# Differential attention in a hybrid diffusion block: a combination split between two engines and placed later, and products with v over two query tiles

## Chip, core and metric

One NeuronCore of a Trainium2 chip runs the whole program. The metric is the device time in microseconds. The engines are TensorE (PE, and PEld for its weight loads), VectorE (DVE), ScalarE (ACT), GpSimd (POOL) and SyncE (SP, which issues most DMAs).

## The reference

Two layers of a transformer block run over 1024 latent tokens and 256 context tokens (model width 1024). Each layer has three parallel head groups, an output projection and a gated MLP. The change lies in the first head group, differential attention: 4 heads, each with two score maps (m = 0, 1) over keys of width 32 and values of width 64.

```python
s = jnp.einsum('bqhmd,bkhmd->bhmqk', qb, keys).astype(F32) * scale
p = jax.nn.softmax(s, axis=-1)
w = p[:, :, 0] - lam * p[:, :, 1]
return jnp.einsum('bhqk,bkhd->bqhd', w.astype(vals.dtype), vals)
```

Latent queries see all 1280 keys. Context queries see the 256 context keys alone, and are needed in layer 0 only. An RMS norm per head follows, so the weights w may carry any common factor of a query.

## The kernel before

`Build.da` (line 860) runs the differential attention of a layer in steps. A step is one head and one tile of 128 queries: 4 heads times 10 tiles, 40 steps, in layer 0 (8 of them small, the context tiles), and 4 times 8, 32 steps, in layer 1. Tiles come in blocks (context tiles 8 and 9; tiles 0 to 3; tiles 4 to 7), heads in two pairs.

One step passes through these functions, with queries on the partitions until the transposes:

- `scores` (L890, matmul L901), once per map: scores of 128 queries against 1280 keys (256 in a small step) go into a PSUM buffer of three banks; there are two such buffers.
- `maximum` (L903, L911) on VectorE reads the buffer and gives the negated row maximum. `exps` (L913, L918) on ScalarE writes the exponentials to SBUF and accumulates their sum; then the PSUM buffer is free.
- `combine` (L922) on VectorE: the reciprocal of the second sum (L929), the ratio (L930), then w = e0 + ratio * e1 over all columns (L931), in place. The result is the difference of the two softmaxes times the first sum, which the norm takes out again.
- `transpose` (L933): TensorE transposes w in chunks of 128 keys (L942), up to four to a PSUM bank, and ScalarE copies each group of up to 512 columns into the tile `da_w` (L943). A large step has groups of 4, 4 and 2 chunks, a small one a single group of 2.
- `products` (L945): for each chunk a matmul with v as weights and the transposed w as 128 moving columns (`pv_mm`, L742); even and odd chunks go to two halves of the partitions of `da_pv`.
- `finish` (L954) calls `pv_combine` (L744): ScalarE copies one half to SBUF (L749) and VectorE adds the other half into the block's output `da_o` (L750). After the last tile of a block's second head `sub_norm` (L1096) starts the norm.

The loop at L963 writes the order by hand: in round n it writes the combination of step n-1, the products of step n-2, the maxima and exponentials of step n, `finish` of step n-2, other work from `plan[n]`, the first scores of step n+1, the transposes of step n-1 and the second scores of step n+1. A scheduler then orders each engine's instructions by priority and readiness, so the order in the trace can differ a little from the written one. Each engine executes its own queue strictly in order.

`fill_plan` (L1008) lays two other kinds of work into the steps: matrix-vector products for the modulation (`mod_units`, L302, L330, L291 to L296) and pieces of the output projection of the third head group (L1040: matmuls L1048 to L1050, ScalarE L1054, and an addition on GpSimd, L1056). These, the transposes, the products and the norm share two PSUM banks (`ps_t`, L205). At two places in a layer `load` fetches q and k of the other head pair by DMAs on GpSimd's queue (L856, L857). GpSimd also computes low-order parts of weights and activations (`lo`, L186) and the norm's power (L1111).

SBUF tiles come from pools: the exponentials from a pool of 7 (tag `x`), the transposed weights `da_w` from one of 6 (tag `wt`), and small work tiles from one of 6 (tag `s5`).

Of the kernel before, what the change touches and what calls it, by code (L numbers as in the profile page):

```python
# [11 lines left out]
F32 = mybir.dt.float32  # L12
F32R = mybir.dt.float32r
AF = mybir.ActivationFunctionType
ALU = mybir.AluOpType
# [6 lines left out]
P = 128  # L22
# [148 lines left out]
class Build:  # L171
# [688 lines left out]
    def da(self, pss, todo):  # L860
# [3 lines left out]
        nc, sp = self.nc, self.sp  # L864
# [20 lines left out]
        ns = len(steps)  # L885
# [17 lines left out]
        def maximum(n, mi):  # L903
            u, ti = steps[n]
            st, b = state[n], u["blk"]
            if mi == 0:
                st["sm"] = sp.tile([P, 8], F32, tag="sm", name="da_sm", bufs=8)
                if u["hd"] == 0 and ti == 0:
                    b["s0"] = sp.tile([P, 4, 2, 2], F32, tag="s0", name="da_s0", bufs=5)
                    b["o"] = self.s5("da_o")  # L910
            nc.vector.tensor_reduce(st["sm"][:, mi:mi + 1], st["s"][mi][:, :b["nkc"]], AX.X, ALU.max, negate=True)  # L911

        def exps(n, mi):  # L913
            u, ti = steps[n]
            st, b = state[n], u["blk"]
            nkc = b["nkc"]
            e = self.x_tile("da_e")
            nc.scalar.activation(e[:, :nkc], st["s"][mi][:, :nkc], AF.Exp, bias=st["sm"][:, mi:mi + 1],  # L918
                                 accum_out=b["s0"][:, ti, u["hd"], mi:mi + 1])
            st["e"].append(e)  # L920

        def combine(n):  # L922

            u, ti = steps[n]
            st, b = state[n], u["blk"]
            sm, (w, e1) = st["sm"], st["e"]
            s01 = b["s0"][:, ti, u["hd"], :]
            nkc = b["nkc"]
            nc.vector.reciprocal(sm[:, 4:5], s01[:, 1:2])  # L929
            nc.vector.scalar_tensor_tensor(sm[:, 5:6], s01[:, 0:1], self.nlam, sm[:, 4:5], ALU.mult, ALU.mult)  # L930
            nc.vector.scalar_tensor_tensor(w[:, :nkc], e1[:, :nkc], sm[:, 5:6], w[:, :nkc], ALU.mult, ALU.add)  # L931

        def transpose(n):  # L933
            u, ti = steps[n]
            st, b = state[n], u["blk"]
            w = st["e"][0]
            wt = st["wt"] = self.wt_tile("da_w", F32)
            for c in range(0, b["nk"], 4):
                n4 = min(4, b["nk"] - c)
                pt = self.ps_t("da_t")  # L940
                for i in range(n4):
                    nc.tensor.transpose(pt[:, P * i:P * i + P], w[:, P * (c + i):P * (c + i) + P], self.ident)  # L942
                nc.scalar.activation(wt[:, P * c:P * (c + n4)], pt[:, :P * n4], AF.Copy)  # L943

        def products(n):  # L945
            u, ti = steps[n]
            st, b = state[n], u["blk"]
            hd, nk = u["hd"], b["nk"]
            pv = st["pv"] = self.ps_t("da_pv")[:, :P]
            for c in range(nk):  # L950
                self.pv_mm(pv, c, nk, loaded[b["pair"]]["v"][:, b["kt0"] + c, 64 * hd:64 * hd + 64],
                           st["wt"][:, P * c:P * c + P])

        def finish(n):  # L954
            u, ti = steps[n]
            b = u["blk"]
            self.pv_combine(u["hd"], state[n]["pv"], b["o"][:, P * ti:P * ti + P], P)
            if u["hd"] == 1 and ti == len(b["tiles"]) - 1:
                late.append(self.sub_norm(b))

        scores(0, 0)
        scores(0, 1)
        for n in range(ns + 2):  # L963
            if n == ns // 4 + 3:
                load(1, (0, 1))
            if n == ns // 2 + 3:
                load(1, (2, 3))
            if n == ns - 10:
                for k in range(2, KE):
                    self.y_load(k, "h")  # L970
            if n == ns - 4:
                self.y_split(2, nc.scalar, nc.gpsimd)
            if n == ns - 3:
                self.y_split(3, nc.scalar, nc.gpsimd)
            prev, new, out = 1 <= n <= ns, n + 1 < ns, n >= 2
            if prev:
                combine(n - 1)
            if out:
                products(n - 2)
            if n < ns:  # L980
                maximum(n, 0)
            if n < ns:
                exps(n, 0)
            if n < ns:
                maximum(n, 1)
            if n < ns:
                exps(n, 1)
            if out:
                finish(n - 2)
            if n < ns:  # L990
                for fn in plan[n]:
                    fn()
            if new:
                scores(n + 1, 0)
            if prev:
                transpose(n - 1)
            if new:
                scores(n + 1, 1)
            late = [g for g in late if next(g, True) is None]
            if n == ns - 2:  # L1000
                self.wo = [self.weight(self.a["wo"][self.l, 0], KE * P)]
# [768 lines left out]
```

## Time and profile before

| what | us |
|---|---|
| runs shown (3): median, lowest, highest | 3108.84, 3102.79, 3114.64 |
| profiled execution: its own time, and its span | 3104.49, 3102.60 |
| differential attention of layer 0 / layer 1, as windows of the span | 480 to 731 / 2127 to 2330 |
| busy over the span: PE, DVE, ACT, POOL | 2845.3, 2109.1, 1457.5, 1497.3 |
| mean granted TensorE clock, as a share of 2.4 GHz | 0.972 |

Engines overlap, so busy times add up to more than the span. A matmul's end is modelled, and matmuls are pipelined, so a busy TensorE is not one at its peak. A row of a group gives line, engine, operation, output <- inputs, shapes, count, then busy us, mean ns of one, and the idle time of the engine just before them with what ended it. A row of the timeline gives start, duration, and in brackets idle time before it. A row of the waits names who waited for whom, the total in us, how often, and the longest.

### The profile page before, as it was taken

The numbers are of one execution on the slowest core, as the hardware profiler recorded it, in microseconds if no ns is written. First come the engines' busy times: TensorE is split into PE (matmuls) and PEld (weight loads), VectorE is DVE, ScalarE is ACT, GpSimd is POOL, SyncE is SP. The second block draws the span as 40 slices with busy tenths as digits, with TensorE's granted clock in tenths as the row PEclk, the third lists the DMA queues.
The fourth block names the chain that finished last, engine by engine and source line by source line (L and its number), as shares of the span: only waits on it lengthen the run. The fifth ranks groups of instructions, "written<-read, shape, count | busy, mean of one in ns | idle before, by whom it ended". The sixth has DMA issues, their size and how long they took to land. (4 is left out here: it accounts for less than half of the span.)

```text
span 3102.6 us, 41077 instructions
## 1 busy us (share of the span) xinstructions
PE 2845.3 (92%) x15194; PEld 2307.3 (74%) x15194; DVE 2109.1 (68%) x2979; ACT 1457.5 (47%) x2442; POOL 1497.3 (48%) x971
## 2 busy tenths in 40 slices
PE   6899798999899999998988989798989799998898
PEld 4798665667688888887877778666767678887676
DVE  6956577875855444457887875767885755555997
ACT  5444367775444333343322454467873444444331
POOL 4645402223455444439561664602323566665981
PEclk9999899999999999999999999899999999999999
DMA  7232816654121121143215331454434122224322
GB/s 251 83 93 68 202 27 228 204 197 149 59 80 67 67 75 67 67 174 118 82 57 206 92 108 52 123 121 146 134 110 166 55 82 82 82 82 163 121 84 82
DMA packets 207577, 349.27 MB, mean 113 GB/s; under 512 B 32784, under 2 KB 112400, under 8 KB 207376
## 3 DMA queue, kind: packets, MB, share of 16 engines
q1 hardware_dynamic: 202768, 331.69, 33.2%
q0 software_dynamic: 4608, 14.95, 2.2%
q8 instruction: 120, 1.97, 0.3%
q14 instruction: 81, 0.66, 0.1%
HBM read 257.19 MB, written 89.39 MB: 112 GB/s over the span
## 5 line engine op out<-in xcount | busy, mean ns | idle before, releaser
L184 ACT ACTIVATE w_r<-w_raw 128x512 fp32r<-128x512 f32 x338 | 212.7, 631 | 449.7 <-PE u_ps L1518 280.1
L1490 POOL TENSOR_TENSOR w_raw<-w_raw 128x512 f32<-128x512 f32 x176 | 250.3, 1427 | 227.5 <-DVE w_r L187 102.8
L187 DVE TENSOR_TENSOR w_r<-w_raw,w_r 128x512 fp32r<-128x512 f32 x206 | 150.4, 732 | 251.5 <-ACT w_r L184 251.4
L187 POOL TENSOR_TENSOR w<-raw,w 128x1024 fp32r<-128x1024 f32 (+2 forms) x62 | 142.9, 2311 | 318.2 <-ACT w L184 207.1
L1517 PE MATMUL u_ps<-a,w_r 128*128 128x512 f32 x704 | 278.6, 396 | 5.3 <-DVE vb L1605 4.2
L1518 PE MATMUL u_ps<-a,w_r 128*128 128x512 f32 x704 | 277.8, 395 | 1.4 <-DVE a L187 1.2
L1519 PE MATMUL u_ps<-a,w_r 128*128 128x512 f32 x704 | 276.2, 392 | 0.0
L187 POOL TENSOR_TENSOR w_r<-w_raw,w_r 128x512 fp32r<-128x512 f32 x132 | 190.4, 1442 | 119.9 <-ACT w_r L184 114.7
L1369 PE MATMUL d_ps<-d_ah,d_b 128*128 128x512 f32 x560 | 223.1, 399 | 22.5 <-DVE xd L1346 11.1
L1370 PE MATMUL d_ps<-d_al,d_b 128*128 128x512 f32 x560 | 222.8, 398 | 9.0 <-DVE d_al L187 9.0
L1371 PE MATMUL d_ps<-d_ah,d_b 128*128 128x512 f32 x560 | 221.8, 396 | 0.7 <-DVE d_b L187 0.7
L911 DVE TENSOR_REDUCE da_sm<-da_s 128x1 f32<-128x1280 f32 (+1 forms) x144 | 195.5, 1368 | 34.1 <-PE da_s L901 32.7
L918 ACT ACTIVATE da_e<-da_s,da_sm 128x1280 f32<-128x1280 f32 (+1 forms) x144 | 177.5, 1235 | 23.7 <-DVE da_sm L911 20.6
L1056 POOL TENSOR_TENSOR oy_x<-oy_x,oy_z 128x426 f32<-128x426 f32 (+3 forms) x48 | 52.7, 1099 | 223.5 <-ACT oy_z L1054 191.7
L1517 PEld LDWEIGHTS u_ps<-a,w_r 128*128 128x128 f32 x704 | 133.8, 190 | 35.0 <-DVE vb L1605 5.7
L1518 PEld LDWEIGHTS u_ps<-a,w_r 128*128 128x128 f32 x704 | 133.9, 190 | 29.5 <-DVE a L187 2.0
L1519 PEld LDWEIGHTS u_ps<-a,w_r 128*128 128x128 f32 x704 | 133.7, 190 | 28.7
L1346 DVE SCALAR_TENSOR_TENSOR xd<-d_ps,mods,xd 128x512 f32<-128x512 f32 x200 | 141.0, 740 | 20.4 <-PE d_ps L1371 20.3
L1369 PEld LDWEIGHTS d_ps<-d_ah,d_b 128*128 128x128 f32 x560 | 107.6, 192 | 48.5 <-issue 9.4
L901 PE MATMUL da_s<-dak,daq 96*128 96x512 f32 (+1 forms) x400 | 125.2, 399 | 17.6 <-ACT da_e L918 17.4
L1605 DVE TENSOR_TENSOR vb<-u_ps,vb 128x512 f32<-128x512 f32 x96 | 66.1, 688 | 98.7 <-PE u_ps L1519 89.1
L1370 PEld LDWEIGHTS d_ps<-d_al,d_b 128*128 128x128 f32 x560 | 108.0, 193 | 32.0 <-DVE d_al L187 10.3
(347 smaller groups left out, 8635.6 us busy)
## 6 DMA issues: line engine op xcount, KB each, us to landing
wmod<-in_wmod SPq DMA_DIRECT2D x96, 512.0 KB, 6.4
w_raw<-in_wu SPq DMA_DIRECT2D x44, 1024.0 KB, 5.4
d_w<-in_wd SPq DMA_DIRECT2D x40, 512.0 KB, 3.9
d_a<-ud SPq DMA_DIRECT2D x40, 512.0 KB, 4.7
ud<-conv SPq DMA_DIRECT2D x22, 640.0 KB, 2.9
ud<-conv SPq DMA_DIRECT2D x22, 512.0 KB, 2.6
raw<-in_wg SPq DMA_DIRECT2D x16, 512.0 KB, 4.3
dak<-qk_da POOLq DMA_DIRECT2D x48, 160.0 KB, 8.1
```

The lines of the kernel that those rows point to most:

```text
L184: self.nc.scalar.activation(out, in_, AF.Copy)
L187: (eng or self.nc.vector).tensor_tensor(out, in_, hi.bitcast(F32), ALU.subtract)
L911: nc.vector.tensor_reduce(st["sm"][:, mi:mi + 1], st["s"][mi][:, :b["nkc"]], AX.X, ALU.max, negate=True)
L918: nc.scalar.activation(e[:, :nkc], st["s"][mi][:, :nkc], AF.Exp, bias=st["sm"][:, mi:mi + 1], accum_out=b["s0"][:, ti, u["hd"], mi:mi + 1])
L1346: nc.vector.scalar_tensor_tensor(x, ps, gate, x, ALU.mult, ALU.add)
L1369: nc.tensor.matmul(ps, bh[:, w], ah[:, m], start=on is None and k == 0, stop=False, **kw)
L1370: nc.tensor.matmul(ps, bh[:, w], al[:, m], start=False, stop=False, **kw)
L1371: nc.tensor.matmul(ps, bl[:, w], ah[:, m], start=False, stop=k == 1, **kw)
L1490: sub = lambda o, a, b, op=ALU.subtract: nc.gpsimd.tensor_tensor(o, a, b, op)
L1517: nc.tensor.matmul(ps, wh[:, s], h, start=new and kk == 0, stop=False, skip_group_check=not new)
L1518: nc.tensor.matmul(ps, wh[:, s], lo, start=False, stop=False, skip_group_check=not new)
L1519: nc.tensor.matmul(ps, wl[:, s], h, start=False, stop=kk == 3, skip_group_check=not new)
```

## The change

The three instructions of `combine` become two functions. `ratio` holds the reciprocal and the ratio. The new `combine` gives VectorE all columns but the last 512 and GpSimd the last 512, as a scaling of e1 and an addition; a small step stays wholly on VectorE. Both are written behind the maxima and exponentials of the following step instead of ahead of them, and the transposes of a step follow one round later. The transposed weights of two neighbouring query tiles lie side by side in one tile (chunks 0 to 7 in `da_w`, the rest in a work tile `da_w2`), so that a matmul of `products` moves 256 columns and serves both tiles; products and `finish` run every second round. The last group of a step's transposes (two chunks) is copied by VectorE instead of ScalarE.

```diff
--- before.py
+++ after.py
@@ -919,48 +919,71 @@
                                  accum_out=b["s0"][:, ti, u["hd"], mi:mi + 1])
             st["e"].append(e)
 
-        def combine(n):
+        def ratio(n):
 
             u, ti = steps[n]
             st, b = state[n], u["blk"]
-            sm, (w, e1) = st["sm"], st["e"]
+            sm = st["sm"]
             s01 = b["s0"][:, ti, u["hd"], :]
-            nkc = b["nkc"]
             nc.vector.reciprocal(sm[:, 4:5], s01[:, 1:2])
             nc.vector.scalar_tensor_tensor(sm[:, 5:6], s01[:, 0:1], self.nlam, sm[:, 4:5], ALU.mult, ALU.mult)
-            nc.vector.scalar_tensor_tensor(w[:, :nkc], e1[:, :nkc], sm[:, 5:6], w[:, :nkc], ALU.mult, ALU.add)
-
-        def transpose(n):
+
+        def combine(n):
+
             u, ti = steps[n]
             st, b = state[n], u["blk"]
-            w = st["e"][0]
-            wt = st["wt"] = self.wt_tile("da_w", F32)
-            for c in range(0, b["nk"], 4):
-                n4 = min(4, b["nk"] - c)
+            w, e1 = st["e"]
+            nkc, c = b["nkc"], st["sm"][:, 5:6]
+            h = nkc - 512 if nkc > 512 else nkc
+            nc.vector.scalar_tensor_tensor(w[:, :h], e1[:, :h], c, w[:, :h], ALU.mult, ALU.add)
+            if h < nkc:
+                nc.gpsimd.tensor_scalar(e1[:, h:nkc], e1[:, h:nkc], c, None, ALU.mult)
+                nc.gpsimd.tensor_tensor(w[:, h:nkc], w[:, h:nkc], e1[:, h:nkc], ALU.add)
+
+        def transpose(n):
+
+            u, ti = steps[n]
+            st, b = state[n], u["blk"]
+            w, nk = st["e"][0], b["nk"]
+            i = ti % 2
+            if i == 0:
+                st["wt"] = [self.wt_tile("da_w", F32)[:, 0:256 * min(nk, 8)].rearrange("p (c q) -> p c q", q=256)]
+                if nk > 8:
+                    st["wt"].append(self.s5("da_w2").rearrange("p (c q) -> p c q", q=256))
+            else:
+                st["wt"] = state[n - 1]["wt"]
+            for c in range(0, nk, 4):
+                n4 = min(4, nk - c)
                 pt = self.ps_t("da_t")
-                for i in range(n4):
-                    nc.tensor.transpose(pt[:, P * i:P * i + P], w[:, P * (c + i):P * (c + i) + P], self.ident)
-                nc.scalar.activation(wt[:, P * c:P * (c + n4)], pt[:, :P * n4], AF.Copy)
+                for k in range(n4):
+                    nc.tensor.transpose(pt[:, P * k:P * k + P], w[:, P * (c + k):P * (c + k) + P], self.ident)
+                dst = st["wt"][c // 8][:, c % 8:c % 8 + n4, P * i:P * i + P]
+                src = pt[:, :P * n4].rearrange("p (c q) -> p c q", q=P)
+                if n4 == 2:
+                    nc.vector.tensor_scalar(dst, src, 1.0, None, ALU.mult)
+                else:
+                    nc.scalar.activation(dst, src, AF.Copy)
 
         def products(n):
+
             u, ti = steps[n]
             st, b = state[n], u["blk"]
             hd, nk = u["hd"], b["nk"]
-            pv = st["pv"] = self.ps_t("da_pv")[:, :P]
+            pv = st["pv"] = self.ps_t("da_pv")[:, :2 * P]
             for c in range(nk):
                 self.pv_mm(pv, c, nk, loaded[b["pair"]]["v"][:, b["kt0"] + c, 64 * hd:64 * hd + 64],
-                           st["wt"][:, P * c:P * c + P])
+                           st["wt"][c // 8][:, c % 8, :])
 
         def finish(n):
             u, ti = steps[n]
             b = u["blk"]
-            self.pv_combine(u["hd"], state[n]["pv"], b["o"][:, P * ti:P * ti + P], P)
+            self.pv_combine(u["hd"], state[n]["pv"], b["o"][:, P * ti - P:P * ti + P], 2 * P)
             if u["hd"] == 1 and ti == len(b["tiles"]) - 1:
                 late.append(self.sub_norm(b))
 
         scores(0, 0)
         scores(0, 1)
-        for n in range(ns + 2):
+        for n in range(ns + 3):
             if n == ns // 4 + 3:
                 load(1, (0, 1))
             if n == ns // 2 + 3:
@@ -972,29 +995,28 @@
                 self.y_split(2, nc.scalar, nc.gpsimd)
             if n == ns - 3:
                 self.y_split(3, nc.scalar, nc.gpsimd)
-            prev, new, out = 1 <= n <= ns, n + 1 < ns, n >= 2
-            if prev:
+
+            out = n >= 4 and n % 2 == 0
+            if out:
+                products(n - 3)
+            if n < ns:
+                maximum(n, 0)
+                maximum(n, 1)
+                exps(n, 0)
+                exps(n, 1)
+            if 1 <= n <= ns:
+                ratio(n - 1)
                 combine(n - 1)
             if out:
-                products(n - 2)
-            if n < ns:
-                maximum(n, 0)
-            if n < ns:
-                exps(n, 0)
-            if n < ns:
-                maximum(n, 1)
-            if n < ns:
-                exps(n, 1)
-            if out:
-                finish(n - 2)
+                finish(n - 3)
             if n < ns:
                 for fn in plan[n]:
                     fn()
-            if new:
+            if n + 1 < ns:
                 scores(n + 1, 0)
-            if prev:
-                transpose(n - 1)
-            if new:
+            if 2 <= n <= ns + 1:
+                transpose(n - 2)
+            if n + 1 < ns:
                 scores(n + 1, 1)
             late = [g for g in late if next(g, True) is None]
             if n == ns - 2:
```

## Rows read from the trace of the kernel before

**Rows 1.** Busy time of each engine (with instruction counts), granted clock and DMA share, both stages.
```profile
core 0: us, PE busy (x) PEld busy (x) DVE busy (x) ACT busy (x) POOL busy (x), PEclk, DMA share, GB/s
480.00:731.00 251.00, 229.18 (x1731) 164.40 (x1733) 199.61 (x292) 191.33 (x371) 75.26 (x62) 0.98 0.60 192
2127.00:2330.00 203.00, 181.63 (x1485) 142.19 (x1483) 168.92 (x216) 163.35 (x296) 60.19 (x59) 0.98 0.47 138
```

**Rows 2.** VectorE's groups by shape, layer 0: busy us, mean ns | idle before, releasers.
```profile
L911 DVE TENSOR_REDUCE da_sm<-da_s 128x1 f32<-128x1280 f32 x64 | 94.7, 1487 | 16.4 <-PE da_s L901 15.7
L931 DVE SCALAR_TENSOR_TENSOR da_e<-da_e,da_sm 128x1280 f32<-128x1280 f32 x32 | 53.3, 1667 | 0.8
L750 DVE TENSOR_TENSOR da_o<-da_pv,pvt 64x128 f32<-64x128 f32 x40 | 11.5, 287 | 11.5 <-ACT pvt L749 10.1
L930 DVE SCALAR_TENSOR_TENSOR da_sm<-da_s,nlam,da_sm 128x1 f32<-128x1 f32 x40 | 11.2, 280 | 0.9
```

**Rows 3.** The same view, stage of layer 1: the combination.
```profile
L931 DVE SCALAR_TENSOR_TENSOR da_e<-da_e,da_sm 128x1280 f32<-128x1280 f32 x32 | 53.2, 1662 | 0.9
```

**Rows 4.** Timeline of VectorE in layer 1, one step: start us, duration us.
```profile
2148.84 0.16 DVE L929 RECIPROCAL da_sm<-da_s 128x1 f32<-128x1 f32 x1
2149.14 0.28 DVE L750 TENSOR_TENSOR da_o<-da_pv,pvt 64x128 f32<-64x128 f32 x1
2149.35 0.20 DVE L930 SCALAR_TENSOR_TENSOR da_sm<-da_s,nlam,da_sm 128x1 f32<-128x1 f32 x1
2149.59 1.55 DVE L931 SCALAR_TENSOR_TENSOR da_e<-da_e,da_sm 128x1280 f32<-128x1280 f32 x1
2151.05 2.88 DVE L911 TENSOR_REDUCE da_sm<-da_s 128x1 f32<-128x1280 f32 x2
2154.08 0.16 DVE L929 RECIPROCAL da_sm<-da_s 128x1 f32<-128x1 f32 x1
```

**Rows 5.** Waits in layer 0: who for whom, total us, times, longest.
```profile
DVE da_sm L911 <- PE da_s L901: 20.3, 23, 2.1
DVE da_sm L929 <- ACT da_e L918: 11.8, 14, 1.8
```

**Rows 6.** Waits in layer 1, the same view.
```profile
DVE da_sm L911 <- PE da_s L901: 12.4, 12, 3.7
DVE da_sm L929 <- ACT da_e L918: 8.1, 8, 1.5
```

**Rows 7.** VectorE's groups of the whole span: prices for the operations added.
```profile
L803 DVE TENSOR_SCALAR sw_w<-sw_t 128x512 f32<-128x512 f32 x32 | 22.0, 686 | 3.9 <-PE sw_t L794 3.9
L803 DVE TENSOR_SCALAR sw_w<-sw_t 128x256 f32<-128x256 f32 x4 | 1.7, 425 | 1.1 <-PE sw_t L794 1.1
L750 DVE TENSOR_TENSOR sw_yo<-sw_pv,pvt 64x384 f32<-64x384 f32 x36 | 20.0, 554 | 32.6 <-ACT pvt L749 32.6
```

**Rows 8.** Groups of ScalarE, then of TensorE, layer 0: group copies, products with v.
```profile
L943 ACT ACTIVATE da_w<-da_t 128x256 f32<-128x256 f32 x39 | 15.0, 386 | 2.5 <-PE da_t L942 2.2
L742 PE MATMUL da_pv<-da_w,v 128*64 128x128 f32 x672 | 46.5, 282 | 4.1 <-ACT da_w L943 3.5
```

**Rows 9.** GpSimd's groups by shape, the whole span.
```profile
L1490 POOL TENSOR_TENSOR w_raw<-w_raw 128x512 f32<-128x512 f32 x176 | 250.3, 1427 | 227.5 <-DVE w_r L187 102.8 <-DMA w_raw<-in_wu 78.0 <-PE c_ps L1530 37.2
L578 POOL TENSOR_SCALAR av<-av 128x1280 f32<-128x1280 f32 x12 | 17.9, 1491 | 60.6 <-DVE av L577 58.8 <-DVE qv L658 1.8
```

**Rows 10.** Timelines of VectorE and GpSimd where the two meet, layer 1.
```profile
2144.41 1.55 DVE L931 SCALAR_TENSOR_TENSOR da_e<-da_e,da_sm 128x1280 f32<-128x1280 f32 x1
2144.60 2.14 POOL L1056 TENSOR_TENSOR oy_x<-oy_x,oy_z 128x342 f32<-128x342 f32 x1 [0.26 <-ACT oy_z L1054]
2151.07 0.92 POOL L1056 TENSOR_TENSOR oy_x<-oy_x,oy_z 128x342 f32<-128x342 f32 x1 [4.33 <-ACT oy_z L1054]
2289.24 3.74 DVE L931 SCALAR_TENSOR_TENSOR da_e<-da_e,da_sm 128x1280 f32<-128x1280 f32 x1
2289.27 2.37 POOL L187 TENSOR_TENSOR yl<-yld,yh 128x1024 fp32r<-128x1024 f32 x1 [2.83 <-PE mod_ps L302]
```

More of the change, by code (lines that the diff above doesn't have):

```diff
@@ L920, in exps @@
             st["e"].append(e)
+        def ratio(n):
+            u, ti = steps[n]
+            st, b = state[n], u["blk"]
+            sm = st["sm"]
+            s01 = b["s0"][:, ti, u["hd"], :]
+            nc.vector.reciprocal(sm[:, 4:5], s01[:, 1:2])
+            nc.vector.scalar_tensor_tensor(sm[:, 5:6], s01[:, 0:1], self.nlam, sm[:, 4:5], ALU.mult, ALU.mult)
         def combine(n):
@@ L925, in combine @@
             st, b = state[n], u["blk"]
-            sm, (w, e1) = st["sm"], st["e"]
-            s01 = b["s0"][:, ti, u["hd"], :]
-            nkc = b["nkc"]
-            nc.vector.reciprocal(sm[:, 4:5], s01[:, 1:2])
-            nc.vector.scalar_tensor_tensor(sm[:, 5:6], s01[:, 0:1], self.nlam, sm[:, 4:5], ALU.mult, ALU.mult)
-            nc.vector.scalar_tensor_tensor(w[:, :nkc], e1[:, :nkc], sm[:, 5:6], w[:, :nkc], ALU.mult, ALU.add)
+            w, e1 = st["e"]
[5 more added lines that the diff above has]
+                nc.gpsimd.tensor_tensor(w[:, h:nkc], w[:, h:nkc], e1[:, h:nkc], ALU.add)
         def transpose(n):
```

## The prediction

> **What bounds the kernel now.** I read the windows first, to see how full each engine is in the two stretches that the change touches. In 480 to 731 us (layer 0) TensorE, VectorE and ScalarE show 229, 200 and 191 us of 251; in 2127 to 2330 us (layer 1) 182, 169 and 163 of 203 [rows 1]. No engine is full: VectorE is idle for 51 and 34 us, 85 us in both, and GpSimd is busy for only 75 and 60. The rest of the span, over 2,600 us, is untouched, so all that the change can do is in these 454 us.
>
> The timeline of VectorE shows what a step costs when nothing goes wrong: from one reciprocal to the next 5.24 us, made of the reciprocal 0.16, the sum of the two halves 0.28, the ratio 0.20, the combination 1.55 and two maxima, 2.88, back to back [rows 4]. There VectorE is the bound, with only small gaps. There are 64 such large steps (32 per layer) and 8 small ones (two context tiles, 256 keys, layer 0 alone); at 5.24 the 64 would take 335 us of the 454, so much time lies outside this pattern.
>
> The waits say what VectorE is late for outside it. Two rows carry the argument: its maxima wait for scores from TensorE, 20.3 and 12.4 us, and the reciprocal that opens the combination waits for the second exponential, 11.8 and 8.1 us [rows 5, 6].
>
> **The change part by part.** The sum is made against the profiled execution's own 3104.49 us (span 3102.60); the median of the runs shown, 3108.84, is 4.35 above it, and that is no part of the sum.
>
> (a) *Work on VectorE.* The combination of a large step shrinks from 1280 to 768 columns. An instruction of the same kind on one element takes 0.20 [rows 4], so 0.20 + 1.35 x 768/1280 = 1.01, a saving of 0.54 us. The third group of transposes (256 columns) is now copied by VectorE: 0.425 [rows 7] against 0.386 on ScalarE [rows 8]. One sum of halves over 256 columns replaces two over 128: between 0.287 [rows 2] and 0.554 for 384 [rows 7] I take 0.42, that is 0.08 less per step. Large step: -0.54 + 0.425 - 0.08 = -0.19, times 64 = -12. A small step pays the copy and keeps the whole combination: 8 x (0.425 - 0.08) = +3. In all **-9 us**, counted in full, since in the undisturbed step VectorE is the bound.
>
> (b) *The combination behind the next maxima.* The reciprocal no longer opens a step just behind its own exponential; two maxima stand in between, 2.88 us [rows 4], more than the longest such wait, 1.8 [rows 5]. The row, 11.8 + 8.1 = 19.9 us, goes. What is late next is the maximum itself: it now stands first in the queue, and while TensorE is late with scores, a combination that is ready waits behind it. Ends 0 and -19.9; I take half, **-10 us**.
>
> (c) *ScalarE and TensorE.* ScalarE loses 0.386 us per large step [rows 8], 64 x 0.386 = 25 us, and one copy in two of those that follow the products; its exponentials end sooner, so score buffers come free sooner. TensorE's products run over as many columns as before, half as many instructions of twice the width. No row shows 256 columns; at twice the time of a record nothing is gained, and if the 46.5 us of product records [rows 8] halved, 23 us of TensorE time would go in layer 0. I take nothing for the products themselves: TensorE's column time is the same. For the waits on scores, 32.7 us, I take a third, **-11 us** (ends 0 and -22: they depend on both engines).
>
> (d) *GpSimd.* Each large step adds a scaling and an addition of 512 columns. The addition costs 1.43 [rows 9]; the scaling is bounded by 0.60 (512/1280 of 1.491) and 1.49 [rows 9], and I take 0.65, nearer the proportional end because the row's work is per column. Together 2.1 us, 64 x 2.1 = 134 us on top of 135: still under 60% of 454, so GpSimd does not become the bound by its load. But the two engines do not run side by side here. A combination that met a running GpSimd addition took 3.74 us instead of 1.55, just its own time after GpSimd's 2.37; an addition that started inside a combination took 2.14 instead of 0.92 [rows 10]. The Trainium skill (SBUF — State Buffer, Who interferes with whom) says the same: a VectorE instruction with two inputs in SBUF and a GpSimd instruction that reads SBUF exclude each other for a whole instruction. The trace agrees, with both numbers above; by the rule the order of the two starts decides, and GpSimd first in half of the steps would bring the sum near the slower rival's below. Before, such meetings lengthened combinations by 106.5 - 64 x 1.55 = 7.3 us [rows 2, 3] and ratios in layer 0 by 40 x 0.08 = 3.2 [rows 2, 4], 10.5 us. GpSimd's load doubles, so another 10.5 us at equal odds. I take half, **+5 us**: behind its share VectorE has two maxima (2.88 us, read from PSUM and of 1.487 us on the mean however GpSimd stands [rows 2]), longer than the pair's 2.1.
>
> (e) *The copy on VectorE is a new wait.* It stands in VectorE's order and waits for TensorE's last transposes; behind it stand the next maxima, and ScalarE waits for those. The nearest rows, the same copy in the windowed attention, idle 3.9 + 1.1 us over 36 [rows 7], 0.14 each, 10 us over 72. Ends 0 and 10; half, **+5 us**, as one maximum in front of it covers it.
>
> (f) *The ends.* Nothing stands behind the last combination of a layer: VectorE's 1.01 and then GpSimd's 2.1 replace 1.55, +1.6 us each, **+3 us** (ends 0 and 3). In the middle of the stage this lateness is hidden by the step now left between combination and transposes; at the four places where GpSimd issues loads of q and k its queue stands still for a few us, and the cover may be gone. No DMA is added or resized.
>
> Sum: -9 - 10 - 11 + 5 + 5 + 3 = **-17 us**, 3104.5 - 17 = 3087.5, about **3087 us**.
>
> **The rivals.** *Only renamed waits* (the change does not do what it says). In the undisturbed step the two maxima already stand back to back, with the reciprocal behind them and hardly a gap [rows 4]: the order written is not what was missing. For it: VectorE's busy time falls by only 9 us. Against it: 20 us of waits for exponentials do exist [rows 5, 6]. Then (b) and (c) are nothing: 3104.5 - 9 + 5 + 5 + 3 = 3108, or 3103 if (e) is hidden; 3106.
>
> *GpSimd goes first* (slower). Ratio and combination are two instructions; where a maximum is put between them, or GpSimd is still at an earlier addition, the pair holds SBUF when VectorE's share or the next ratio comes. One such step costs about the addition, 1.43 us [rows 9]. Without (d) and (e) the gain is 27 us, so it turns into a loss from 27/1.43 = 19 of the 64 steps on; at 35 of them 3104.5 - 27 + 50 = 3127. For it: the 3.74 us case [rows 10]. Against it: an idle GpSimd gets the ratio's signal no earlier than VectorE, whose combination follows in 0.04 us [rows 4]. A second rule of the Trainium skill (GPSIMD Engine Reference, Engine selection) speaks against the split as such, elementwise work with two inputs being about twice as slow there; here 2.1 us replace 0.54, and it matters only by this rival.
>
> *The slack opens the stage.* With a step between combination and transposes both waits go, (b) -20 and (c) -22: 3104.5 - 9 - 20 - 22 + 5 + 5 + 3 = 3066. For it: three engines at 76 to 91% that only wait for each other [rows 1].
>
> **How the numbers follow.** Chances: forecast 0.42 (own range 3072 to 3100), only renamed 0.26, GpSimd first 0.18, slack 0.14. The range takes in the slack case down to 3052 and most of the slow one: 3052 to 3122. A difference under 0.5%, 15.5 us, can't be told from none. Faster by more means under 3089: three quarters of the forecast's case, 0.32, the slack case, 0.14, and 0.02 of the second: 0.48. Slower by more is over 3120: 0.16, nearly all of the slower case. Within: the rest, 0.36.
>
> **What would show it.** Right: combinations near 1.0 us, the reciprocal's wait for exponentials under 3 us, undisturbed steps near 5.0, and both stages together some 17 us shorter. (c) is wrong if the maxima's waits for scores stay over 30 us; (d) if the mean combination exceeds 1.2 or the ratio 0.35; (e) if VectorE idles over 10 us before its new copies. If GpSimd shows long additions and transposes wait for it, the chain through GpSimd has become the bound and the forecast fails.

## The result, and the profile after

| | kernel before | changed kernel |
|---|---|---|
| median of 4 runs, us | 3108.12 (3102.79 to 3114.64) | 3135.70 (3135.02 to 3142.56) |
| ratio, 95% interval | | 1.0096 (1.0077 to 1.0115) |
| span of the profiled execution | 3102.6 | 3133.7 |
| stage of layer 0: first maximum to last sum | 479.0 to 737.0 = 258.0 | 477.9 to 759.1 = 281.2 |
| of it from the start of the last maximum | 13.1 | 18.5 |
| stage of layer 1 | 2121.7 to 2336.5 = 214.8 | 2140.8 to 2367.8 = 226.9 |
| of it from the start of the last maximum | 13.6 | 19.3 |

The change made the kernel about 1% slower, 30 us by the ratio, where 17 us less had been forecast; 3135.7 lies outside the range. The timelines of VectorE give the ends of the stages: they are 23 and 12 us longer, 35 together, and the span grew by 31: all of the loss is there, and the rest of the program is 4 us shorter. That is a reading of single executions: the rest, which the kernels below leave alone (but for work added on GpSimd that ran there), took 2611 to 2640 us in their profiled executions, 2630 before and 2626 after, so stages compare to some 10 us. "Stage" below means these two stretches, "drain" the part of one from the start of its last maximum.

The windows of the changed kernel over most of the two stages [rows 1]:

```profile
core 0: us, PE busy (x) PEld busy (x) DVE busy (x) ACT busy (x) POOL busy (x), PEclk, DMA share, GB/s
480.00:750.00 270.00, 238.37 (x1391) 156.15 (x1389) 199.56 (x307) 174.21 (x308) 174.03 (x126) 0.91 0.56 181
2143.00:2360.00 217.00, 193.93 (x1199) 135.75 (x1199) 169.07 (x234) 156.24 (x258) 167.85 (x126) 0.92 0.46 136
```

VectorE is as busy as before (199.6 and 169.1 us against 199.6 and 168.9) in stretches 19 and 14 us longer. ScalarE has been relieved, GpSimd has gone from 75 and 60 to 174 and 168 us, and TensorE's granted clock has fallen from 0.98 to 0.91 and 0.92.

VectorE's and GpSimd's groups of the changed kernel, whole span [rows 2, 3, 7, 9]:

```profile
L911 DVE TENSOR_REDUCE da_sm<-da_s 128x1 f32<-128x1280 f32 x128 | 189.8, 1486 | 30.8 <-PE da_s L901 29.7
L938 DVE SCALAR_TENSOR_TENSOR da_e<-da_e,da_sm 128x768 f32<-128x768 f32 x64 | 71.6, 1119 | 2.2
L963 DVE TENSOR_SCALAR da_w<-da_t 128x256 f32<-128x256 f32 x72 | 30.0, 417 | 16.6 <-PE da_t L959 16.1
L929 DVE SCALAR_TENSOR_TENSOR da_sm<-da_s,nlam,da_sm 128x1 f32<-128x1 f32 x72 | 25.8, 359 | 2.2
L750 DVE TENSOR_TENSOR da_o<-da_pv,pvt 64x256 f32<-64x256 f32 x36 | 15.1, 420 | 24.8 <-ACT pvt L749 24.4
L928 DVE RECIPROCAL da_sm<-da_s 128x1 f32<-128x1 f32 x72 | 11.3, 157 | 20.2 <-ACT da_e L918 19.9
...
L940 POOL TENSOR_SCALAR da_e<-da_e,da_sm 128x512 f32<-128x512 f32 x64 | 121.6, 1901 | 67.7 <-DVE da_sm L929 37.7 <-ACT mod_m L330 7.6 <-ACT yh L184 6.3
L941 POOL TENSOR_TENSOR da_e<-da_e 128x512 f32<-128x512 f32 x64 | 89.1, 1393 | 4.2
```

Two things are to be seen. The reciprocal (L928) still waits 19.9 us for exponentials, as before. And GpSimd's scaling (L940) takes 1.90 us on the mean, longer than the addition of two inputs beside it. The waits of the stage of layer 0, then of layer 1 [rows 5, 6]:

```profile
ACT da_e L918 <- DVE da_sm L911: 21.5, 26, 2.6
PEld da_s L901 <- ACT da_e L918: 21.2, 23, 2.4
DVE da_sm L911 <- PE da_s L901: 20.7, 25, 2.6
POOL da_e L940 <- DVE da_sm L929: 17.6, 11, 3.5
DVE da_sm L928 <- ACT da_e L918: 10.8, 11, 1.7
DVE da_w L963 <- PE da_t L959: 8.4, 8, 2.3
```
```profile
POOL da_e L940 <- DVE da_sm L929: 20.1, 15, 5.0
DVE da_sm L911 <- PE da_s L901: 14.2, 14, 2.4
DVE da_sm L928 <- ACT da_e L918: 9.1, 11, 1.5
DVE da_w L963 <- PE da_t L959: 6.8, 2, 5.8
```

The two waits that the change was to shorten stand at 34.9 us (maxima for scores, 32.7 before) and 19.9 (reciprocals for exponentials, 19.9 before). Nothing is gone, and new waits have come beside them: VectorE's copy for transposes, 15.2 us.

The drain of layer 0 shows how an end lengthens. The windows of the changed kernel, then a part of TensorE's timeline there:

```profile
736.00:740.00 4.00, 2.74 (x17) 1.81 (x15) 3.87 (x8) 2.96 (x6) 3.92 (x3) 1.00 0.33 127
740.00:743.00 3.00, 1.06 (x5) 1.07 (x6) 3.00 (x4) 2.77 (x5) 2.92 (x2) 0.79 0.00 0
743.00:747.00 4.00, 4.00 (x18) 3.82 (x18) 3.06 (x6) 1.73 (x4) 4.00 (x3) 0.50 0.35 95
```
```profile
737.65 1.09 PE L959 MATMUL da_t<-cst_all,da_e 128*128 128x128 f32 x8 [0.80 <-DVE da_o L750]
...
741.93 1.86 PE L1127 MATMUL sub_c<-cst_all,osq 128*128 128x2 f32 x8 [2.38 <-ACT osq L1124]
743.66 1.95 PE L959 MATMUL da_t<-cst_all,da_e 128*128 128x128 f32 x8
...
747.39 2.95 PE L742 MATMUL da_pv<-da_w,v 128*64 128x256 f32 x20
750.28 0.66 PE L959 MATMUL da_t<-cst_all,da_e 128*128 128x128 f32 x4
751.35 0.87 PE L959 MATMUL da_t<-cst_all,da_e 128*128 128x128 f32 x6
753.23 0.60 PE L959 MATMUL da_t<-cst_all,da_e 128*128 128x128 f32 x4
754.37 0.82 PE L959 MATMUL da_t<-cst_all,da_e 128*128 128x128 f32 x6
```

The last maximum starts at 740.6. Three steps' transposes still follow (743.66, 750.28, 753.23). Before, it started at 723.9 and two did (TensorE's timeline of the kernel before):

```profile
727.00 0.63 PE L942 MATMUL da_t<-cst_all,da_e 128*128 128x128 f32 x4 [1.34 <-DVE da_e L931]
728.73 0.87 PE L942 MATMUL da_t<-cst_all,da_e 128*128 128x128 f32 x6
...
731.90 0.66 PE L942 MATMUL da_t<-cst_all,da_e 128*128 128x128 f32 x4
733.26 0.86 PE L942 MATMUL da_t<-cst_all,da_e 128*128 128x128 f32 x6
```

In the changed kernel TensorE has nothing to do for 2.38 us, after that its granted clock is 0.50 (the 1.2 GHz level), and eight transposes take 1.95 us instead of 1.09. The mean clocks say how often that happens: (1 - 0.91) x 2 x 270 = 49 and (1 - 0.92) x 2 x 217 = 35 us at the lower level, against 10 and 8 before, where the clock was 0.98.

### The profile page after: what moved, and what is told of

It is laid out like the page before. It is cut to its first block, busy times and chain, and to the rows that moved or that the text cites. A ratio compares the mean times of both kernels' runs of the same rounds, so it can differ in the third digit from the quotient of the medians.

```text
span 3133.7 us, 39861 instructions
## 1 busy us (share of the span) xinstructions
PE 2871.4 (92%) x14538; PEld 2298.5 (73%) x14538; DVE 2109.7 (67%) x3015; ACT 1433.6 (46%) x2336; POOL 1712.6 (55%) x1099
## 3 DMA queue, kind: packets, MB, share of 16 engines
q1 hardware_dynamic: 202768, 331.69, 32.7%
## 5 line engine op out<-in xcount | busy, mean ns | idle before, releaser
L911 DVE TENSOR_REDUCE da_sm<-da_s 128x1 f32<-128x1280 f32 (+1 forms) x144 | 196.5, 1368 | 36.3 <-PE da_s L901 34.9
L918 ACT ACTIVATE da_e<-da_s,da_sm 128x1280 f32<-128x1280 f32 (+1 forms) x144 | 177.8, 1236 | 50.9 <-DVE da_sm L911 34.4
L940 POOL TENSOR_SCALAR da_e<-da_e,da_sm 128x512 f32<-128x512 f32 x64 | 121.6, 1901 | 67.7 <-DVE da_sm L929 37.7
L660 POOL TENSOR_TENSOR qr<-qv,mhalf 128x8 f32<-128x8 f32 (+2 forms) x40 | 108.0, 2704 | 51.3 <-DVE qv L658 50.7
```

## The experiments

The suspects at the start: GpSimd's share (its instructions that shut VectorE's out of SBUF, and its late part of the weights), the new order, the pairs of tiles, the copy on VectorE. "us" behind a ratio is (ratio - 1) x 3104. No run leaves a part of the computation out.

### One part of the change taken back

**Combination whole on VectorE again** (r1):

```diff
-            h = nkc - 512 if nkc > 512 else nkc
+            h = nkc
```

> The changed kernel with the whole combination on VectorE again (no GpSimd share). GpSimd theory (the scaling and the addition, 1.90 + 1.36 us a large step, make the weights late and keep GpSimd's queue busy): about 3100 us, at least 25 us faster than the changed kernel's 3136, with combinations of 1.55 us. Order theory, pairing theory and copy theory (the part that costs is another one): VectorE gets 64 x 0.5 = 32 us more work, and the time is 3136 or more.

3131.7 us, 1.0086 (1.0057 to 1.0114). Only 3 us of the 30 are gone, which the intervals can't tell from none: inside the change the split is not what sets the time, as long as the rest stays.

**The old order of the rounds** (r2), split, pairs and copy kept:

```diff
+            if 1 <= n <= ns:
+                ratio(n - 1)
+                combine(n - 1)
             if out:
-                products(n - 3)
+                products(n - 2)
...
-            if 2 <= n <= ns + 1:
-                transpose(n - 2)
+            if 1 <= n <= ns:
+                transpose(n - 1)
```

> The changed kernel with the old order of a round: combination ahead of the maxima, transposes of step n-1, products one round earlier; split, pairing and copy stay. Order theory (the late combination makes ready work wait behind maxima that wait for scores, and lengthens the end of a layer): about 3110 us, and the stretch from the last maximum to the last output some 5 us shorter in each layer. GpSimd theory: slower still than 3136, since the transposes of a step now wait for GpSimd's pair with no round in between: 3150 or more. The others: 3136 within 8.

3122.61 us, 1.0057 (1.0034 to 1.0079): 12 us back, and the drains are 13.4 and 13.0 us again. So the order costs, though it was to bring the gain.

**Products one tile at a time** (r3): `da_pv` of 128 columns, `da_w` per step, products in every round.

> The changed kernel with products for one query tile at a time, every round, 128 columns; split, order and copy stay. Pairing theory (products of two rounds in one burst leave TensorE idle in the other round, and its clock falls): about 3115 us, and less time at half clock in the two stages than the changed kernel's 85 us. The others: 3136 to 3145, as the copies and sums of halves double in number (72 instead of 36).

3151.99 us, 1.0150 (1.0126 to 1.0173). The pairs are no culprit: without them the rest is 17 us slower still.

**The last group copied by ScalarE** (r4): `if n4 == 2` becomes `if False`.

> The changed kernel with the copy of the last group of transposes on ScalarE again. Copy theory (VectorE's queue holds a PSUM bank longer, TensorE waits): about 3120 us. The others: 3136 within 8.

3121.94 us, 1.0060 (1.0044 to 1.0077): 11 us back.

### One part alone on the kernel before

**Pairs alone** (s1), **copy alone** (s2):

> The kernel before with one part of the change: products over two query tiles at once (transposed weights of a pair side by side, sums of halves over 256 columns); order, combination and copy as before. If the parts add up as the four single reversals say (pairing was worth 16 us there), 3088 us, faster than both kernels. If pairing only helps where the transposes are late, as in the new order, 3104 within 6.

> The kernel before with one part of the change: the last group of transposes copied by VectorE. If the copy's price is its own (VectorE's queue lengthens by 0.42 us a step and holds a PSUM bank longer): 3116 to 3130. If it only hurts beside the other parts: 3104 within 6.

3110.41 us, 1.0017 (1.0008 to 1.0027), and 3108.54 us, 1.0007 (0.9997 to 1.0017): 5 us, at the upper end of the second forecast for s1, and nothing that can be told from none for s2.

**Split alone** (s3), `combine` as in the change, at its old place; **order alone** (s4), the rounds as in the change, without split, pairs or copy:

> The kernel before with one part of the change: GpSimd takes the last 512 columns of the combination. GpSimd theory with the old order: the transposes of the same round wait for a pair of 1.6 and 1.3 us behind the combination, and the time is 3120 or more. If GpSimd's share is as harmless as in the changed kernel (4 us worth when taken out there): 3104 within 8, or faster by up to 15 for the 0.54 us a step that VectorE saves.

> The kernel before with one part of the change: the combination behind the next maxima, transposes and products one round later. Order theory: 3115 to 3125, of which 5 us a layer between the last maximum and the last output. If the order only hurts beside the other parts: 3104 to 3114.

3129.57 us, 1.0077 (1.0062 to 1.0092), and 3125.42 us, 1.0067 (1.0052 to 1.0082). Each of the two costs more than 20 us alone: 24 + 21 + 5 + 2 = 52, where the whole change costs 30. So the parts don't add up; they cover each other in part. Split and pairs together (s5):

> The kernel before with split and pairing, without the new order and without the copy. If the new order is what makes the split bearable: 3130 or more, above the 3122 of the changed kernel with the copy on ScalarE. If the order buys the split nothing: 3115 or less.

3129.40 us, 1.0087 (1.0066 to 1.0109): 27 us, a hair under the 3130 of the first forecast, and close to the sum of the two, 24 + 5.

With r2, r4 and the changed kernel this makes a square of four kernels that all hold split and pairs. In the old order they cost 27 us without the copy (s5) and 18 with it (r2, which also writes both maxima ahead of the exponentials, as the new order does); in the new order 19 without it (r4) and 30 with it (the changed kernel). So the copy takes off 9 us in the old order and adds 11 in the new one, and the new order adds 12 with the copy and nothing without it. A difference of 8 or 9 us is at the edge of these intervals; the change of sign, 20 us from corner to corner (0.0066, with an interval of 0.0040 if the four are combined as independent), is clear of them.

### What of the order costs

**Only the combination later** (o1): the combination is written behind the maxima and exponentials of the next step; transposes and products stay in their rounds.

```diff
-            if prev:
-                combine(n - 1)
...
                 exps(n, 1)
+            if 1 <= n <= ns:
+                combine(n - 1)
```

> The kernel before with the combination written behind the next maxima, while transposes and products stay in their old rounds. If what costs in the new order is the combination standing behind maxima that wait for scores: 3118 or more. If it is the round by which the transposes are later: 3106 within 6.

3105.89 us, 1.0006 (0.9993 to 1.0019): moving the combination does nothing.

**Only the transposes later** (o2): combination in place, transposes and products one round later.

```diff
...
-            if prev:
-                transpose(n - 1)
+            if 2 <= n <= ns + 1:
+                transpose(n - 2)
```

> The kernel before with transposes and products one round later and the combination where it was. If the later transposes are what costs in the new order: 3118 to 3125, with some 5 us more between the last maximum and the last output of each layer. If it is the place of the combination: 3106 to 3112.

3116.61 us, 1.0039 (1.0022 to 1.0056): 12 us, with drains of 18.1 and 17.9. In the kernel's own timelines the mean time from the end of VectorE's combination to the first transpose of its step is, in the large steps, 5.6 us before, 11.3 after and 11.8 with the order alone (s4). That round is what the order really moves.

**The changed kernel with its transposes in the old round** (q2), and **the same without the split** (q3):

```diff
...
-            if 2 <= n <= ns + 1:
-                transpose(n - 2)
+            if 1 <= n <= ns:
+                transpose(n - 1)
```

> The changed kernel, with the transposes of a step written in the round after its maxima, as before, instead of one round later; products and sums follow one round earlier with them. If the later round of the transposes is the part of the order that costs, the ends of the layers come back to about 13 us and the time falls by 5 to 14 us against the changed kernel, to 3120 to 3130; the rival, that the split alone now sets the time and covers it, has no fall: 3133 to 3138.

> As the run before it, and the combination left whole on VectorE: of the change, the combination behind the maxima, the pairs of tiles and VectorE's copy remain. With both suspected costs gone the theory (later transposes 13 to 20 us, share of GpSimd 24) has only the pairs' 5 and the copy's 2 left: 3104 to 3115 us. If the cost lies in the pairs and the copy together with the new place of the combination, it stays over 3120.

3126.3 us, 1.0062 (1.0041 to 1.0084), and 3105.34 us, 1.0003 (0.9992 to 1.0014). With both taken out, the later combination, the pairs and the copy remain and the loss is gone from the time. (In its profiled execution the two stages are 482 us, still 9 longer than before, and the rest 10 shorter.) From there the changed kernel can be built up again: the split adds 1.0062 - 1.0003, 18 us, the later transposes 1.0096 - 1.0062, another 11. Without the split the later transposes add 1.0086 - 1.0003, 26 us. That is one way to add the loss up; by the square above it is split and pairs 27, and copy and order together 3. One thing that the later round gives back beside the split is to be seen on TensorE's transposes in q2 and in the changed kernel:

```profile
L959 PE MATMUL da_t<-cst_all,da_e 128*128 128x128 f32 x656 | 107.0, 290 | 15.8 <-POOL da_e L941 7.8 <-ACT oy_z L1076 2.3 <-DVE da_sm L928 2.1
```
```profile
L959 PE MATMUL da_t<-cst_all,da_e 128*128 128x128 f32 x656 | 101.9, 282 | 7.0 <-DVE da_w L963 2.0 <-ACT oy_z L1076 1.7 <-DVE mods L293 1.0
```

In the old round the transposes wait 7.8 us for GpSimd's addition; one round later no such wait is left. The order does what it is for, and with the copy it costs more than that.

### What of GpSimd's share costs

**The same load on a tile that nobody reads** (o3): combination whole on VectorE, in each large step a scaling by the ratio and two additions of 320 columns added, work of no use:

```diff
...
+            if nkc > 512:
+                nc.gpsimd.tensor_scalar(scr, scr, sm[:, 5:6], None, ALU.mult)
+                nc.gpsimd.tensor_tensor(scr, scr, scr, ALU.add)
+                nc.gpsimd.tensor_tensor(scr, scr, scr, ALU.add)
```

> The kernel before, whole combination on VectorE, with three more GpSimd instructions behind each large step's ratio (a scaling and two additions of 320 columns, about as long together as the pair of the split) on a tile that nothing else reads. Theory of the path (the split costs because the transposes wait for GpSimd's late half): 3106 to 3112. Theory of the port and the queue (GpSimd's instructions shut VectorE's combination out of SBUF and hold up GpSimd's own work): 3120 or more, with combinations of 1.8 us on the mean or longer.

3127.68 us, 1.0081 (1.0061 to 1.0101), with combinations of 1.78 us on the mean: as much as the split alone, though nothing waits for these results. The lateness of the weights is not needed for the loss.

**The wait without the load** (q4): of the three instructions only the scaling, of one column.

> The kernel before, with one scaling of a single column by the ratio added on GpSimd to each large step, its result unread. It has the wait for the ratio in GpSimd's queue, and almost none of the load. If the cost of the share is that GpSimd stands still behind a wait for VectorE, some 10 to 24 us are to be seen; if it is the work itself (port and busy time), under 5 us: 3099 to 3109.

3100.06 us, 0.9985 (0.9973 to 0.9997): no cost. Two places in GpSimd's and VectorE's timelines of q4 show how the two engines take turns:

```profile
2153.55 1.57 POOL L935 TENSOR_SCALAR scr<-scr,da_sm 128x1 f32<-128x1 f32 x1 [2.96 <-DVE da_sm L932]
...
2160.12 0.28 POOL L935 TENSOR_SCALAR scr<-scr,da_sm 128x1 f32<-128x1 f32 x1 [3.50 <-DVE da_sm L932]
```
```profile
2153.41 1.55 DVE L933 SCALAR_TENSOR_TENSOR da_e<-da_e,da_sm 128x1280 f32<-128x1280 f32 x1
...
2159.97 1.49 DVE L913 TENSOR_REDUCE da_sm<-da_s 128x1 f32<-128x1280 f32 x1
```

One column takes 0.28 us beside a maximum, which reads PSUM, and 1.57 beside a combination, until that ends.

**A load that reads nothing** (q1), eight fills of a work tile like o3's; and, because two thirds of those ran outside the stages, a **pair tied to its step** (q5, q6): two fills, or two scalings by 1.0, of the second exponential tile once the combination has read it.

```diff
+            if nkc > 512:
+                nc.gpsimd.memset(e1[:, :nkc], 0.0)
+                nc.gpsimd.memset(e1[:, :nkc], 0.0)
```
```diff
+            if nkc > 512:
+                nc.gpsimd.tensor_scalar(e1[:, :nkc], e1[:, :nkc], 1.0, None, ALU.mult)
+                nc.gpsimd.tensor_scalar(e1[:, :nkc], e1[:, :nkc], 1.0, None, ALU.mult)
```

> The kernel before, with eight fills of a 128x320 work tile on GpSimd added to each large step; nothing reads the tile, so this is work of no use. It stands beside the run with a scaling and two additions of the same tile, which came out 24 us slower. If what costs is that VectorE and GpSimd read SBUF in turn (a fill reads nothing; the Trainium skill, SBUF — State Buffer, Who interferes with whom, has a GpSimd instruction that only writes not contend with VectorE's second input), this comes out within 0.3% of the kernel before, 3096 to 3112 us, with the mean combination near its 1.67 us. If it costs because GpSimd's queue is fuller and its other work (weight parts, output sums) comes later, it comes out 10 to 25 us slower if the fills take 2 us or more a step.

> The kernel before, with two fills by GpSimd of all 1280 columns of a large step's second exponential tile once the combination has read it; nothing reads them. They are tied to their step, which the fills of the work tile were not (two thirds of those ran outside the two stages), and read nothing from SBUF. If the cost of GpSimd's share is that the two engines read SBUF in turn, this comes within 0.3% of the kernel before, 3095 to 3113 us, though GpSimd carries some 2.8 us a step. If GpSimd's busy time and the later release of the tile cost, it is 10 to 25 us slower, as its twin.

> The twin of the run before it: two scalings by 1.0 of the same 1280 columns in place of the two fills, some 2.6 us a step, at the same place; the one difference is that GpSimd reads SBUF. If reading in turn costs, this is 10 to 25 us slower than the kernel before and than its twin, with longer ratios and combinations on VectorE; if GpSimd's busy time costs, both are slower alike; if neither, both stay within 0.3%.

q1: 3102.7 us, 0.9992 (0.9977 to 1.0006), but only 61 of its 187 us of fills fell into the stages, so it tells little. q5: 3114.42 us, 1.0030 (1.0019 to 1.0040). q6: 3325.01 us, 1.0701 (1.0676 to 1.0726). VectorE's groups before, then GpSimd's and VectorE's of q5, of q6 and GpSimd's of o3:

```profile
L931 DVE SCALAR_TENSOR_TENSOR da_e<-da_e,da_sm 128x1280 f32<-128x1280 f32 x64 | 106.5, 1664 | 1.7
...
L930 DVE SCALAR_TENSOR_TENSOR da_sm<-da_s,nlam,da_sm 128x1 f32<-128x1 f32 x72 | 18.1, 251 | 1.5
```
```profile
L934 POOL MEMSET da_e<- 128x1280 f32 x64 | 74.7, 1169 | 2.1
...
L931 DVE SCALAR_TENSOR_TENSOR da_e<-da_e,da_sm 128x1280 f32<-128x1280 f32 x64 | 103.8, 1622 | 2.8
L930 DVE SCALAR_TENSOR_TENSOR da_sm<-da_s,nlam,da_sm 128x1 f32<-128x1 f32 x72 | 19.2, 267 | 1.6
```
```profile
L934 POOL TENSOR_SCALAR da_e<-da_e 128x1280 f32<-128x1280 f32 x64 | 236.1, 3690 | 3.3
...
L931 DVE SCALAR_TENSOR_TENSOR da_e<-da_e,da_sm 128x1280 f32<-128x1280 f32 x64 | 148.0, 2312 | 2.9
L930 DVE SCALAR_TENSOR_TENSOR da_sm<-da_s,nlam,da_sm 128x1 f32<-128x1 f32 x72 | 73.6, 1022 | 1.6
```
```profile
L935 POOL TENSOR_SCALAR scr<-scr,da_sm 128x320 f32<-128x320 f32 x64 | 122.1, 1907 | 66.7 <-DVE da_sm L932 61.4 <-DVE amul L346 2.9 <-DVE sub_v L1114 1.2
L936 POOL TENSOR_TENSOR scr<-scr 128x320 f32<-128x320 f32 x64 | 53.4, 835 | 4.3
```

The pair is not as even as meant: the scalings took 3.4 us each at the shortest, not 1.3, so q6 carries three times q5's load, and its 7% can't be set against q5 one to one. But q5 and o3 have nearly the same load of their own, 2 x 1.17 = 2.34 us a step against 1.08 + 2 x 0.72 = 2.52 (the shortest scaling and addition in o3), and differ in reading: 9 us against 25, though q5 also gives back the tile later. Fills leave VectorE's combination and ratio alone (103.8 + 19.2 = 123.0 us, before 106.5 + 18.1 = 124.6); scalings stretch them to 148.0 + 73.6 = 221.6. If VectorE's instructions in the stages are sorted by line, tiles and shape, and for each kind the time above its lower quartile is added up, the sums (its stretch) are 21 us before, 17 in q5, 17 in q3, 37 in o3, 33 in q2 and 35 after. That is 16 us more in o3 than before and 4 less in q5. So reading in turn would account for some 15 us of o3's 25, if all of VectorE's lost time reaches the end; the 9 us that fills cost too may be GpSimd's busy time or the later tile, which no run separates. The Trainium skill (SBUF — State Buffer, Who interferes with whom) states it so: VectorE with two inputs in SBUF contends with a GpSimd instruction that reads SBUF, not with one that only writes. The runs agree, with the numbers above.

## Why the prediction was wrong

(a) *VectorE's prices* were right: combinations of 1.01 us where undisturbed, 0.417 for the copy (0.425 said), 0.420 for the sum (0.42 said). Some 10 us of work did go, but the stretched ratios took most of it back: combination 71.6 - 106.5, copy +30.0, sums 15.1 - 20.7, ratios 25.8 - 18.1, in all -2.8 us over the whole span. VectorE being the bound in an undisturbed step didn't help: before, only 21 of the 70 intervals from one reciprocal to the next are under 5.35 us.

(b) *The combination behind the next maxima: the step that failed first.* 10 of 19.9 us were to go, because the reciprocal "no longer opens a step just behind its own exponential". In the trace before it did not do that either: in 48 of 72 steps a maximum of the following step already ran ahead of the reciprocal, since the scheduler orders by readiness. After, in 40 of 72; and the two maxima that were to stand in between stood ahead of the reciprocal in only 7 (before, in none). The wait is 19.9 us in both, and o1 alone is 1.0006. For (b) and (c) this is the rival that only renames waits. That its 3106 lies near q3's 3105.34 is no proof of its sum, which holds the split and the ends too.

(c) *Waits on scores*, a third of 32.7 us: 34.9 after. ScalarE was relieved as said, from 355 to 330 us in the windows, but its exponentials then waited 34.4 us for maxima, 20.6 before, and the waits for scores did not fall. Products over 256 columns took 408 ns against 280 for 128 ([rows 8]: 282 in layer 0), so 85.2 us in all for 89.5; nothing of weight was to be had there.

(d) *GpSimd's share, +5 forecast: the largest miss in size among the costs.* The scaling was put at 0.65 us by the columns of another row; it takes 1.55 at least and 1.90 on the mean, above the upper bound of 1.49. The pair takes 1.90 + 1.39 = 3.29 us, longer than the two maxima (2.88) that were to hide it. That the two engines take turns was told right in kind, though it cost nearly three times the 5 us: VectorE's stretch grew from 21 to 35 us. Of the signs named for it, the ratio came (0.36 us, over 0.35), the combination did not (1.12, under 1.2). (In [rows 10] the combination ends 1.34 us behind GpSimd's addition, a little less than its own 1.55.) The split as a whole costs 18 us with the transposes in the old round, 24 alone. How these divide inside the change between the stretch, the late half of the weights and TensorE's lower clock isn't separated; o3 shows that the load suffices, q4 that the wait alone doesn't.

(e) *The copy's wait*: 15.2 us after, above the upper end of 10. But the idle time before the copy is not its price. The copy costs nothing alone (s2); with split and pairs in the old order it takes off 9 us (s5 to r2), although VectorE idles 25.7 us for it there:

```profile
L963 DVE TENSOR_SCALAR da_w<-da_t 128x256 f32<-128x256 f32 x72 | 30.1, 418 | 25.9 <-PE da_t L959 25.7
```

In the new order it adds 11 us (r4 to the changed kernel), with 16.1 us of such idle time. What makes it dear one round later is open.

(f) *The ends, +3 forecast*: 5.4 and 5.7 us. The combination's own lateness was counted; that the transposes of three steps still stand behind the last maximum was not. More, the prediction took the step left between combination and transposes as cover at no price. It has a price in four pairs of kernels: 11 us beside split and copy (q2 to the changed kernel), 26 without the split (q3 to r1), 12 in o2, 19 between o1 and s4. In a fifth, with the split and without the copy (s5 to r4), it has none: 8 us less, although r4's drains, 22.5 and 18.7 us, are together 11 longer than s5's. So the price depends on which parts stand beside it, and how is open. In the changed kernel the drains explain some 11 us. Beyond them stand ScalarE's waits for maxima (28.1 us in q3, 36.6 in r1) and the lower clock: the time at the lower level, worked out as above over the whole stages, is 17 us before, 32 in q3, 55 in q2, 73 in r1 and 83 after. Both are company and not a cause shown: no run set the clock apart.

*The rivals.* Slower was given 0.16. The mechanism of "GpSimd goes first" is real, as the ratios show (0.73 and 0.42 us instead of 0.20 in the changed kernel's steps where a GpSimd instruction holds SBUF), but it alone doesn't reach 3135; no case had the transposes' round as a price. No kernel with a part of the change beats the one before; the best of them (o1, q3) can't be told from it.

The timelines of VectorE and GpSimd in the changed kernel hold one such meeting:

```profile
2188.69 0.42 DVE L929 SCALAR_TENSOR_TENSOR da_sm<-da_s,nlam,da_sm 128x1 f32<-128x1 f32 x1
2189.04 0.41 DVE L750 TENSOR_TENSOR da_o<-da_pv,pvt 64x256 f32<-64x256 f32 x1
2189.37 1.00 DVE L938 SCALAR_TENSOR_TENSOR da_e<-da_e,da_sm 128x768 f32<-128x768 f32 x1
```
```profile
2187.53 1.56 POOL L941 TENSOR_TENSOR da_e<-da_e 128x512 f32<-128x512 f32 x1
2189.28 2.52 POOL L940 TENSOR_SCALAR da_e<-da_e,da_sm 128x512 f32<-128x512 f32 x1 [0.19 <-DVE da_sm L929]
```

The ratio is held until the addition of the step before ends at 2189.09; the scaling, started just ahead of the combination, takes 2.52 us instead of the 1.57 that it takes at 2185.45.

## What to carry to other kernels

Before a reordering is priced, count in the trace how often the order that it is to mend is really there: with a scheduler between, the written place of an instruction may change nothing, and what changes is the round in which its consumers stand. Work moved to GpSimd beside a VectorE that reads two operands from SBUF costs more by what GpSimd reads than by how busy it is (25 us against 9 at nearly the same load here), whatever its idle share; price it by the same form of instruction, and try the load on an unread tile before building on it. Slack between stages isn't free: it is paid at each end of the loop, and whether the middle gives it back depends on the other parts. Parts of a change tried alone need not add up (52 us against 30 here), and one can change its sign beside another, as the copy did; so try them in pairs before calling one the culprit.

## What the runs showed of the hardware

GpSimd's scaling with one operation is slow: 0.28 us for one column, 1.08 for 320, 1.55 for 512 and 3.44 for 1280 (the shortest in q4, o3, the changed kernel and q6), that is (3.44 - 1.08)/960 = 2.5 ns a column, the same with a per-partition factor and with a constant. The row taken as its price (L578, [rows 9]) has two operations with constants over 1280 columns and takes 1.26 at the shortest, 1 ns a column. Fills of 1280 columns took 1.17 us.
